# Two more units of dense matmuls ahead of the transposes of the widest attention row block, seven more ahead of the cumulative sum of the SSD decays

## The chip, the cores and the metric

The kernel runs on one core of a Trainium2 chip. The metric is the time of one execution in microseconds of the device. Before the change, three runs took 1780.59, 1785.44 and 1792.77 us; the median is 1785.44 us.

## The reference, cut to what matters

One decoder block on 512 tokens plus 16 meta tokens, width 2048. After an RMSNorm, one input projection gives q, k, v, a gate, the inputs of a state-space branch (z, x, B, C, dt) and two merge gates. Two branches run on these: differential attention with ALiBi over 8 heads, and a chunked state-space scan (SSD). They are projected, merged by gates, projected again, added to the input and normalised. The two places that this case is about:

```python
def diff_attention(q, k, v, lam):            # 8 heads, blocks of 128 rows
    ...
        s = s - (slopes[:, None, None] * dist)[None, :, None]
        s = jnp.where(valid, s, NEG)
        p = jax.nn.softmax(s, axis=-1)
        a = p[:, :, 0] - lam * p[:, :, 1]     # two maps, subtracted
        return jnp.einsum('bhqk,bkhe->bqhe', a, vf)
...
    dtf = jax.nn.softplus(dt + dt_bias[l])
    a = -jnp.exp(a_log[l])
    da = dt * a ; acs = jnp.cumsum(da, axis=-1)   # within chunks of 128, in ssd_chunked
```

## The kernel before, in words

**Dense work.** All large matrix products are cut into jobs. A job loads four weight tiles (128x1024), and most jobs use one level of Strassen: seven products P1, P6, P7, P4, P2, P3, P5 with two *units* each, so 14 units. A unit is 12 matmuls of 256 or 264 columns: each weight block is split into a high part `wh` (ACT, L194) and a rest `wl` (DVE, `split`, L190), and the products are high by high, high by low and low by high. `wh` and `wl` have five buffers each. The units go through a short pipeline: sums of weights, then the split, then, three units later (`LOOK`, L391), the matmuls.

**Side work.** Attention and the SSD scan are Python generators in the list `tasks`. After each dense unit, `run_side` (L218) advances each active generator to its next `yield`, so one `yield` is one unit of dense work between two steps. At most three are active, and a new one starts at least three units after the last one during attention. A head makes seven tasks: the transposes of v, the parts of q and k, four row blocks (`attn_rows`, i = 0 to 3; the widest, i = 3, spans 528 keys), and `attn_out`, which squares, scales and transposes the output that the row blocks left in `o_ps`. The next head's tasks follow 28 units (two jobs) behind.

**A row block** computes its scores, biases them with a running minimum (DVE), takes the two exponentials (ACT, L789), combines the two maps into `a` (DVE, L793 to L796; the tile's name in the profile is `sc`), waits three yields, and transposes `a` on TensorE (L803 to L806; `s_ps<-ident,sc`). `at` and `ax` are copied out of PSUM, and one yield later `o_ps` is accumulated.

**decays** (L917) is the only side task of the stage that projects B, C and x and runs the convolution (the conv stage, from about 577 us on). It turns dt into `dtk` by a softplus written as a series on DVE (tiles `eac`, `dec`, `dds`, `acs` of 128x160), forms `da` (stored in `dec`, L956), waits five yields, and sums it with two matmuls against `tri` and `ones` (L963, L964). In this stage each job also has conv taps on DVE (`cv<-raw`, L995; `cv<-cth`, L998).

**Order.** TensorE executes in the order in which the program is written (`InOrder`). VectorE is held to it only for the first units (`setattr(dve, "on", False)`, L698). After that the scheduler of the tile framework chooses the order of DVE, ACT, POOL and the queue SP; each engine then works off its list in order and stops at the first instruction whose inputs are missing. Weight tiles, the constants of the next stage and stores all go through SP.

Of the kernel before, what the change touches and what calls it, by code (L numbers as in the profile page):

```python
# [137 lines left out]
def block_kernel(ctx, tc, t_in, out):  # L138
# [12 lines left out]
    def side_ps():  # L151
        return pss.tile([P, 512], F32, tag="s", bufs=4, name="s_ps")
# [17 lines left out]
    for _, _, form, mat, _ in jobs:  # L170
        n = 2 if form == "A" else {"att": 2, "dt": 1}.get(mat, 4)
# [566 lines left out]
    def attn_rows(hd, i, qs, ks, kl, vt, hs):  # L738

        slope = 2.0 ** -(hd + 1)  # L740
        n = M + (i + 1) * P
        n0 = min(n, 512)
        to = P * (3 - i)
        if i == 0:
            hs["sm"] = ab.tile([P, 2, NT], F32, tag="sm", bufs=2, name="sm")
            hs["o"] = pso.tile([P, NT, P], F32, tag="o", bufs=1, name="o_ps")
        sm, o_ps = hs["sm"], hs["o"]
        mn = ab.tile([P, 4], F32, tag="mn", bufs=3, name="mn")
        pr, pq = [], {}

        def scores(*maps):
            rows = slice(i * P, (i + 1) * P)
            todo = []
            for m in maps:
                pq[m] = [side_ps(), side_ps() if n > n0 else None]
                todo += [(m, ps, a, b) for ps, a, b in ((pq[m][0], 0, max(n0, 256)), (pq[m][1], n0, n))
                         if ps is not None]
            for m, ps, a, b in todo:
                pe.matmul(ps[:, :b - a], lhsT=qs[:, m, rows], rhs=ks[:, m, a:b], start=True, stop=False)
            for m, ps, a, b in todo:  # L760
                ms = slice(64 * m, 64 * m + 64)
                pe.matmul(ps[:, :b - a], lhsT=qs[ms, m, rows], rhs=kl[ms, a:b], start=False, stop=True)

        def biased(m):
            s_ = ab.tile([P, L], F32, tag="sc", bufs=SC, name="sc")
            dve.tensor_tensor_reduce(out=s_[:, :n0], in0=pq[m][0][:, :n0], in1=tb[:, to:to + n0], scale=1.0,
                                     scalar=FAR, op0=ALU.add, op1=ALU.min, accum_out=mn[:, m:m + 1])
            if n > n0:
                dve.tensor_tensor_reduce(out=s_[:, n0:n], in0=pq[m][1][:, :n - n0], in1=tb[:, to + n0:to + n], scale=1.0,
                                         scalar=FAR, op0=ALU.add, op1=ALU.min, accum_out=mn[:, 2 + m:3 + m])  # L770
            pr.append(s_)

        if n == n0:
            scores(0, 1)
            yield
            biased(0)
        else:
            scores(0)
            yield
            biased(0)  # L780
            scores(1)
            yield
        biased(1)
        if n > n0:
            dve.tensor_tensor(mn[:, 0:2], mn[:, 0:2], mn[:, 2:4], ALU.min)
        dve.tensor_scalar(mn[:, 0:2], mn[:, 0:2], slope, None, ALU.mult)
        yield
        for m in range(2):
            act.activation(pr[m][:, :n], pr[m][:, :n], AF.Exp, scale=-slope, bias=mn[:, m:m + 1],  # L789
                           accum_out=sm[:, m, i:i + 1])  # L790
        yield
        cc = ab.tile([P, 1], F32, tag="cc", bufs=2, name="cc")
        dve.reciprocal(cc, sm[:, 1, i:i + 1])  # L793
        dve.scalar_tensor_tensor(cc, cc, nlam, sm[:, 0, i:i + 1], ALU.mult, ALU.mult)
        a = pr[0]
        dve.scalar_tensor_tensor(a[:, :n], pr[1][:, :n], cc, a[:, :n], ALU.mult, ALU.add)  # L796
        yield
        yield
        yield
        at = ab.tile([P, 4, P], F32, tag="at", bufs=1, name="at")  # L800
        ax = ab.tile([M, P], F32, tag="ax", bufs=1, name="ax")
        ps = side_ps()
        for j in range(i + 1):  # L803
            pe.transpose(ps[:, j * P:(j + 1) * P], a[:, j * P:(j + 1) * P], ident)
        pa = ps[:M, 3 * P:] if i < 3 else side_ps()[:M, :P]
        pe.transpose(pa, a[:, (i + 1) * P:n], ident)  # L806
        yield
        act.activation(at[:, :i + 1, :], ps[:, :(i + 1) * P], AF.Copy)
        dve.tensor_copy(ax, pa)
        yield  # L810
        for j in range(i + 1):
            pe.matmul(o_ps[:, i, :], lhsT=at[:, j, :], rhs=vt[:, j, :], start=(j == 0), stop=False)
        pe.matmul(o_ps[:, i, :], lhsT=ax, rhs=vt[:M, i + 1, :], start=False, stop=True)
        yield

    def attn_out(hd, sg, hs):

        for _ in range(6):
            yield
        sm, o_ps = hs["sm"], hs["o"]  # L820
        ssq = ab.tile([P, NT], F32, tag="ssq", bufs=2, name="ssq")
        r0 = ab.tile([P, NT], F32, tag="r0", bufs=2, name="r0")
        og = ab.tile([P, NT, P], F32, tag="at", bufs=1, name="og")
        for i in range(NT):
            act.activation(og[:, i, :], o_ps[:, i, :], AF.Square, accum_out=ssq[:, i:i + 1])
        dve.reciprocal(r0, sm[:, 0, :])
        yield
        dve.tensor_tensor(ssq, ssq, r0, ALU.mult)
        dve.tensor_tensor(ssq, ssq, r0, ALU.mult)
        dve.tensor_scalar(ssq, ssq, 1.0 / P, EPS, ALU.mult, ALU.add)  # L830
        pool.tensor_tensor(ssq, ssq, mhalf[:, :NT], ALU.pow)  # L831
        yield
        yield
        dve.tensor_tensor(r0, r0, ssq, ALU.mult)
        dve.tensor_tensor(og, o_ps, r0.unsqueeze(2).to_broadcast([P, NT, P]), ALU.mult)
        yield
        yield
        ps = side_ps()
        for i in range(NT):
            pe.transpose(ps[:, i * P:(i + 1) * P], og[:, i, :], ident)  # L840
        yield
        dve.scalar_tensor_tensor(sg, ps, gat, sg, ALU.mult, ALU.mult)
        sp.dma_start(d_oa[hd % 2, :, :, hd // 2].rearrange("t p n -> p t n"), sg.rearrange("p (t n) -> p t n", t=2))
        yield
# [15 lines left out]
    def head_tasks(hd, qT, kT, vT, vt, sg):  # L860
        hs = {}
        qs = ab.tile([P, 2, S], F32R, tag="qs", bufs=1, name="qs")
        ks = ab.tile([P, 2, L], F32R, tag="ks", bufs=1, name="ks")
        kl = ab.tile([P, L], F32R, tag="kl", bufs=1, name="kl")
        tasks.append(v_tokens(vT, vt))
        tasks.append(qk_parts(hd, qT, kT, qs, ks, kl))
        for i in range(NT):
            tasks.append(attn_rows(hd, i, qs, ks, kl, vt, hs))
        tasks.append(attn_out(hd, sg, hs))
# [47 lines left out]
    def decays(sb):  # L917
# [36 lines left out]
        act.activation(al, al, AF.Exp)  # L954
        da = e5
        dve.scalar_tensor_tensor(da, dtk, -1.0, al.unsqueeze(1).to_broadcast([P, 5, 32]), ALU.mult, ALU.mult)  # L956
        yield
        yield
        yield
        yield  # L960
        yield
        ps = side_ps()
        pe.matmul(ps[:, :160], lhsT=tri, rhs=da, start=True, stop=True)  # L963
        pe.matmul(ps[:, 160:320], lhsT=ones.to_broadcast([P, P]), rhs=da, start=True, stop=True)  # L964
# [17 lines left out]
    with tc.tile_pool(name="conv", bufs=2) as sb:  # L982
# [23 lines left out]
        def conv_job(ji, fts):  # L1006
# [11 lines left out]
            return strassen(ji, HL, 0, dst, fin)  # L1018

        tasks.append(decays(sb))  # L1020
        for g in range(NG):
            dense(conv_job(job_at["bc", g], [16 + g, 20 + g]))
# [448 lines left out]
```

## Time and profile before

| | before |
|---|---|
| median of three runs | 1785.44 us (1780.59 to 1792.77) |
| the profiled execution | 1787.64 us, of which the span of its instructions 1785.9 us |
| TensorE busy | 1677.5 us (94%) |
| VectorE busy | 1556.6 us (87%) |
| ScalarE busy | 962.8 us (54%) |
| granted TensorE clock, mean | 0.982 |

Busy times overlap, so they don't add up to the span. The attention stage lies at about 125 to 575 us, the conv stage at about 577 to 862 us. The waits view lists for an engine what it stood idle for; the timeline shows single instructions with the idle time before them; the windows view gives the busy time of each engine in a stretch, with the granted clock (1.00 is 2.4 GHz, 0.50 is 1.2 GHz).

### The profile page before, as it was taken

To read this page: it belongs to the slowest core of one execution; us is meant where nothing else is said; L and a number is where in the kernel's file an instruction comes from. 1 tells how busy PE (TensorE), PEld (TensorE's weight loads), DVE (VectorE), ACT (ScalarE), POOL (GpSimd) and SP (SyncE) were. 2 spreads that over 40 slices of the span, in tenths; PEclk is the share of its full clock that TensorE was granted. 3 is DMA by queue.
4 is the path that set the end of the run, shared out by engine and by line. 5 is a ranking of instruction groups with operands and counts; after the bars stand their busy time and mean duration, and the time that the engine had idled before them with its cause. 6 is when DMAs were issued, how large, how long until landed. Compare 5 with 4: busy or idle time off the path is not lost. (4 is left out here: it accounts for less than half of the span.)

```text
span 1785.9 us, 35840 instructions
## 1 busy us (share of the span) xinstructions
PE 1677.5 (94%) x13547; PEld 1622.2 (91%) x13547; DVE 1556.6 (87%) x3016; ACT 962.8 (54%) x1957; POOL 243.9 (14%) x232
## 2 busy tenths in 40 slices
PE   4999999999999799999899989999999999989996
PEld 3999988889889799999898988999998999989996
DVE  6789878888888899999798988989987499999997
ACT  5455555555565455555556656665564254456553
POOL 0000000000000000000013232323300022223443
PEclk8999999999999899999999999999999999999998
DMA  7342222222223333333455555554467544533433
GB/s 305 107 129 73 90 89 77 72 79 88 89 91 112 100 120 122 129 120 130 148 166 157 174 159 169 163 178 146 150 231 247 189 132 163 170 125 112 141 119 107
DMA packets 136765, 244.10 MB, mean 137 GB/s; under 512 B 15088, under 2 KB 78768, under 8 KB 136080
## 3 DMA queue, kind: packets, MB, share of 16 engines
q1 hardware_dynamic: 136592, 241.81, 41.9%
q8 instruction: 107, 1.75, 0.4%
q14 instruction: 66, 0.54, 0.1%
HBM read 207.88 MB, written 33.88 MB: 135 GB/s over the span
## 5 line engine op out<-in xcount | busy, mean ns | idle before, releaser
L128 PE MATMUL d_ps<-x,wh 128*128 128x256 f32 (+1 forms) x4896 | 912.9, 287 | 15.1 <-DVE cth L128 4.3
L128 PEld LDWEIGHTS d_ps<-x,wh 128*128 128x128 f32 x4896 | 764.4, 191 | 31.9 <-issue 9.3
L128 PE MATMUL d_ps<-x,wl 128*128 128x256 f32 (+1 forms) x2448 | 698.6, 285 | 17.0 <-DVE wl L128 16.5
L194 ACT ACTIVATE wh<-w 128x512 fp32r<-128x512 f32 x706 | 437.4, 627 | 395.2 <-PE d_ps L128 299.2
L128 PE MATMUL d_ps<-y,wh 128*128 128x256 f32 (+1 forms) x3216 | 600.0, 286 | 9.1 <-ACT wh L194 4.6
L128 DVE TENSOR_TENSOR wl<-w,wh 128x512 fp32r<-128x512 f32 x706 | 505.4, 727 | 105.1 <-ACT wh L194 99.6
L128 PEld LDWEIGHTS d_ps<-y,wh 128*128 128x128 f32 x3216 | 498.1, 190 | 20.3 <-issue 5.5
L128 PEld LDWEIGHTS d_ps<-x,wl 128*128 128x128 f32 x2448 | 464.9, 190 | 22.5 <-DVE wl L128 22.0
L128 PE MATMUL d_ps<-y,wl 128*128 128x256 f32 (+1 forms) x1608 | 455.7, 283 | 4.9 <-DVE wl L128 4.9
L128 PEld LDWEIGHTS d_ps<-y,wl 128*128 128x128 f32 x1608 | 303.9, 189 | 6.3 <-DVE wl L128 6.3
L194 ACT ACTIVATE wh<-S 128x512 fp32r<-128x512 f32 x260 | 160.6, 627 | 193.0 <-PE d_ps L128 111.5
L128 DVE TENSOR_TENSOR wl<-S,wh 128x512 fp32r<-128x512 f32 x260 | 182.9, 719 | 26.8 <-ACT wh L194 24.7
L128 DVE TENSOR_TENSOR S<-S,w 128x512 f32<-128x512 f32 x130 | 93.2, 753 | 0.0
L128 DVE TENSOR_TENSOR w<-w 128x512 f32<-128x512 f32 x130 | 90.8, 715 | 0.0
L128 DVE TENSOR_TENSOR w<-w,S 128x512 f32<-128x512 f32 x130 | 89.4, 699 | 0.9
L128 DVE TENSOR_TENSOR S<-w 128x512 f32<-128x512 f32 x130 | 86.3, 705 | 2.1 <-DMA w<-in_w_all 2.0
L211 POOL TENSOR_TENSOR mq<-mq,cth 128x256 f32<-128x256 f32 x32 | 43.7, 1379 | 260.8 <-ACT wh L194 144.7
L831 POOL TENSOR_TENSOR ssq<-ssq,mhalf 128x4 f32<-128x4 f32 x8 | 8.1, 1007 | 470.7 <-DVE ssq L128 470.7
L128 DVE TENSOR_TENSOR u<-d_ps,u 128x256 f32<-128x256 f32 (+1 forms) x130 | 55.2, 424 | 9.3 <-PE d_ps L128 8.8
L1117 ACT ACTIVATE mm<-mm,acs 128x128 f32<-128x128 f32 x128 | 40.1, 389 | 36.8 <-DMA mm<-d_acs 36.8
L128 DVE SCALAR_TENSOR_TENSOR cv<-raw,c_conv_w,cv 128x528 f32<-128x528 f32 x72 | 54.5, 779 | 1.1 <-issue 0.7
L211 POOL TENSOR_TENSOR state<-state,dec 128x512 f32<-128x512 f32 x12 | 19.6, 1630 | 172.3 <-DVE state L128 172.2
(233 smaller groups left out, 1524.1 us busy)
## 6 DMA issues: line engine op xcount, KB each, us to landing
w<-in_w_all SPq DMA_DIRECT2D x291, 512.0 KB, 3.6
mm<-d_acs SPq DMA_DIRECT2D x16, 512.0 KB, 6.5
d_x<-cv SPq DMA_DIRECT2D x24, 264.0 KB, 2.0
q_B<-in_xT SPq DMA_DIRECT2D x8, 528.0 KB, 11.9
d_tha<-gth SPq DMA_DIRECT2D x16, 256.0 KB, 2.4
lx<-d_x SPq DMA_DIRECT2D x16, 256.0 KB, 4.2
ea<-d_acs SPq DMA_DIRECT2D x32, 128.0 KB, 3.7
d_sz<-gth SPq DMA_DIRECT2D x16, 256.0 KB, 4.1
```

The source lines that it names most:

```text
L128: r = op(*args, **kw)
L194: act.activation(h[:, :n], src, AF.Copy)
L211: pool.tensor_tensor(dst, a, b, ALU.mult)
L831: pool.tensor_tensor(ssq, ssq, mhalf[:, :NT], ALU.pow)
L1117: act.activation(mm[:, h, :], mm[:, h, :], AF.Relu, scale=-1.0, bias=acs[:, c, g * HPG + h:g * HPG + h + 1])
```

## The change

Three numbers of yields change. In `attn_rows`, the row block i = 3 (the only one with `n > n0`) waits five units instead of three between the combination of the maps and the transposes. `attn_out` begins two units later, so that its squares stay behind the last write of `o_ps`. In `decays`, 12 units instead of 5 lie between `da` and the two matmuls. No instruction is added or taken away.

```diff
@@ attn_rows
         dve.scalar_tensor_tensor(a[:, :n], pr[1][:, :n], cc, a[:, :n], ALU.mult, ALU.add)
-        yield
-        yield
-        yield
+        for _ in range(5 if n > n0 else 3):
+            yield
@@ attn_out
-        for _ in range(6):
+        for _ in range(8):
             yield
@@ decays
         dve.scalar_tensor_tensor(da, dtk, -1.0, al.unsqueeze(1).to_broadcast([P, 5, 32]), ALU.mult, ALU.mult)
-        yield
-        yield
-        yield
-        yield
-        yield
+        for _ in range(12):
+            yield
```

What this does to the order of instructions, at three places:

TensorE, second head, around the transposes of its row block 3 (`s_ps` is the transposes' PSUM tile, `sc_2628` the combined map, `d_ps` a product of a dense unit). Before:

```order
L128 MATMUL d_ps_2747<-x_542,wh_2696 128x256
L128 MATMUL d_ps_2747<-x_541,wl_2697 128x256
L128 MATMUL s_ps_2782<-ident_139,sc_2628 128x128 x4
L128 MATMUL s_ps_2787<-ident_139,sc_2628 16x128
L128 MATMUL d_ps_2794<-x_100,wh_2725 128x264
```

Now:

```order
L128 MATMUL d_ps_2785<-x_101,wh_2743 128x264
L128 MATMUL d_ps_2785<-x_100,wl_2744 128x264
L128 MATMUL s_ps_2819<-ident_139,sc_2628 128x128 x4
L128 MATMUL s_ps_2824<-ident_139,sc_2628 16x128
L128 MATMUL d_ps_2834<-y_623,wh_2764 128x264
```

The 24 matmuls of 264 columns that read `wl_2726` and `wl_2744` stood behind the transposes and now stand ahead of them. This is the same in the heads after it.

VectorE, at the same place, up to the instruction that completes `sc_2628`. Before:

```order
L128 TENSOR_SCALAR mn_2601<-mn_2601 128x2
L128 TENSOR_TENSOR u4_2761<-d_ps_2700,u2_2547 128x256
L128 TENSOR_TENSOR wl_2765<-S_2741,wh_2764 128x512
L128 TENSOR_TENSOR wl_2791<-S_2741,wh_2790 128x512
L128 TENSOR_TENSOR sg_1961<-d_ps_2747,u3_2597 128x256
L128 TENSOR_TENSOR qT_1957<-d_ps_2747,u4_2761 128x256
L128 RECIPROCAL r0_2834<-sm_2338 128x4
L128 RECIPROCAL cc_2720<-sm_2338 128x1
L128 SCALAR_TENSOR_TENSOR cc_2720<-cc_2720,nlam_151,sm_2338 128x1
L128 TENSOR_TENSOR wl_2813<-w_2470,wh_2812 128x512
L128 SCALAR_TENSOR_TENSOR sc_2628<-sc_2664,cc_2720,sc_2628 128x528
```

Now:

```order
L128 TENSOR_SCALAR mn_2601<-mn_2601 128x2
L128 TENSOR_TENSOR u4_2761<-d_ps_2700,u2_2547 128x256
L128 TENSOR_TENSOR wl_2765<-S_2741,wh_2764 128x512
L128 RECIPROCAL r0_2875<-sm_2338 128x4
L128 RECIPROCAL cc_2720<-sm_2338 128x1
L128 TENSOR_TENSOR sg_1961<-d_ps_2747,u3_2597 128x256
L128 TENSOR_TENSOR qT_1957<-d_ps_2747,u4_2761 128x256
L128 SCALAR_TENSOR_TENSOR cc_2720<-cc_2720,nlam_151,sm_2338 128x1
L128 TENSOR_TENSOR wl_2782<-S_2741,wh_2781 128x512
L128 SCALAR_TENSOR_TENSOR sc_2628<-sc_2664,cc_2720,sc_2628 128x528
```

One split fewer stands between the scaled minimum `mn` and `sc`; on ScalarE the two exponentials of L789 stand one split earlier, right behind `wh_2764`. The heads after it show the same; the first head's order is unchanged here.

VectorE in the conv stage, the end of the softplus series up to `dec` (this is `da`) and what follows it. Before:

```order
L128 SCALAR_TENSOR_TENSOR dtk_7369<-acs_7370,dtk_7369 128x160
L128 SCALAR_TENSOR_TENSOR cv_7767<-raw_7640,c_conv_w_7377,cv_7767 128x528
L128 SCALAR_TENSOR_TENSOR cv_7815<-raw_7593,c_conv_w_7377,cv_7815 128x528
L128 COPY eac_7371<-dtk_7369 128x32
L128 SCALAR_TENSOR_TENSOR cv_7767<-cth_7768,cv_7767 128x528
L128 MEMSET dtk_7369 128x32
L128 SCALAR_TENSOR_TENSOR cv_7815<-cth_7816,cv_7815 128x528
L128 COPY dtk_7369<-eac_7371 16x32
L128 SCALAR_TENSOR_TENSOR dec_7372<-dtk_7369,c_a_log_7365 128x160
L128 COPY acs_7370<-s_ps_7699 128x160
```

Now, the last of it:

```order
L128 MEMSET dtk_7369 128x32
L128 SCALAR_TENSOR_TENSOR cv_7799<-cth_7800,cv_7799 128x528
L128 TENSOR_TENSOR wl_7854<-w_7492,wh_7853 128x512
L128 TENSOR_TENSOR S_7921<-w_7742,w_7744 128x512 x2
L128 COPY dtk_7369<-eac_7371 16x32
L128 TENSOR_TENSOR wl_7874<-w_7492,wh_7873 128x512
L128 TENSOR_TENSOR w_7742<-w_7578,w_7742 128x512 x2
L128 SCALAR_TENSOR_TENSOR dec_7372<-dtk_7369,c_a_log_7365 128x160
L128 COPY acs_7370<-s_ps_7849 128x160
```

From the sums `raw_7593` and `raw_7640`, which end the stage's first job, up to `dec`, the list had 3 splits `wl` and now has 10; it had no sum of weights (`S`, `w`) and now has 6; and it has 2 sums `u` more. Conv taps and steps of the series are the same. On TensorE the two matmuls that read `dec` stand 84 matmuls (7 units) further back; the last unit ahead of them reads `wl_7624` before and `wl_7765` now.

## Rows read from the trace of the kernel before

**Rows 1.** Waits of PE, 125 to 575 us: total us, times, longest.

```profile
PE s_ps L128 <- DVE sc L128: 17.0, 7, 2.6
```

**Rows 2.** Windows, 125 to 575 us: length, busy PE, PEld, DVE, ACT, POOL, clock, DMA.

```profile
125.00:575.00 450.00, 432.96 (x3393) 410.47 (x3392) 381.13 (x944) 249.82 (x569) 8.54 (x14) 0.99 0.27 87
```

**Rows 3.** Timeline of PE, first and second head: start, us, instruction, idle before.

```profile
176.13 0.76 PE L128 MATMUL s_ps<-ident,sc 128*128 128x128 f32 x5 [1.52 <-DVE sc L128]
...
230.59 0.77 PE L128 MATMUL s_ps<-ident,sc 128*128 128x128 f32 x5 [2.59 <-DVE sc L128]
```

**Rows 4.** Timeline of DVE, second head.

```profile
229.77 0.76 DVE L128 SCALAR_TENSOR_TENSOR sc<-sc,cc 128x528 f32<-128x528 f32 x1
...
234.03 0.69 DVE L128 TENSOR_TENSOR wl<-w,wh 128x512 fp32r<-128x512 f32 x1 [1.53 <-ACT wh L194]
```

**Rows 5.** Timeline of ACT, second head.

```profile
226.54 0.63 ACT L194 ACTIVATE wh<-S 128x512 fp32r<-128x512 f32 x1 [0.78 <-DVE wl L128]
227.08 0.72 ACT L789 ACTIVATE sc<-sc,mn 128x528 f32<-128x528 f32 x1
```

**Rows 6.** Windows behind the waits of the second, third and fourth head.

```profile
231.00:237.00 6.00, 6.00 (x38) 5.77 (x36) 2.74 (x5) 2.14 (x4) 0.00 (x0) 0.72 0.19 49
286.00:292.00 6.00, 5.47 (x33) 5.39 (x34) 3.07 (x6) 2.07 (x4) 0.00 (x0) 0.72 0.00 0
343.00:349.00 6.00, 6.00 (x49) 5.76 (x47) 2.93 (x7) 3.28 (x12) 0.00 (x0) 1.00 0.27 85
```

**Rows 7.** Windows of the conv stage.

```profile
580.00:600.00 20.00, 20.00 (x168) 19.82 (x167) 18.45 (x42) 10.17 (x21) 0.00 (x0) 1.00 0.36 121
600.00:611.00 11.00, 1.24 (x7) 1.05 (x6) 9.54 (x23) 3.48 (x6) 0.20 (x2) 0.68 0.27 92
611.00:620.00 9.00, 9.00 (x65) 8.95 (x64) 3.84 (x8) 3.81 (x8) 0.00 (x0) 0.83 0.26 76
...
640.00:860.00 220.00, 213.75 (x1749) 211.48 (x1747) 219.26 (x424) 116.78 (x198) 1.81 (x18) 1.00 0.37 127
```

**Rows 8.** Waits of PE, 575 to 870 us.

```profile
PE s_ps L128 <- DVE dec L128: 9.8, 1, 9.8
PE d_ps L128 <- DVE wl L128: 6.9, 8, 1.5
```

**Rows 9.** Timeline of PE, the matmuls of `decays`.

```profile
582.33 0.44 PE L128 MATMUL s_ps<-ident,dtx 32*16 32x32 f32 x5
...
600.09 0.28 PE L128 MATMUL d_ps<-x,wl 128*128 128x264 f32 x1
610.14 0.87 PE L128 MATMUL s_ps<-dec,tri 128*128 128x160 f32 x2 [9.76 <-DVE dec L128]
```

**Rows 10.** Timeline of DVE ahead of `dec` and behind it.

```profile
597.37 0.69 DVE L128 TENSOR_TENSOR wl<-w,wh 128x512 fp32r<-128x512 f32 x1
597.97 1.29 DVE L128 TENSOR_TENSOR S<-S,w 128x512 f32<-128x512 f32 x2
599.17 0.43 DVE L128 TENSOR_TENSOR u<-d_ps,u 128x264 f32<-128x264 f32 x1
600.41 0.50 DVE L128 TENSOR_TENSOR raw<-d_ps,u 128x8 f32<-128x8 f32 x2 [0.57 <-PE d_ps L128]
...
609.67 0.33 DVE L128 SCALAR_TENSOR_TENSOR dec<-dtk,c_a_log 128x160 f32<-128x160 f32 x1
...
635.44 2.13 DVE L128 SCALAR_TENSOR_TENSOR cv<-raw,c_conv_w,cv 128x528 f32<-128x528 f32 x3 [0.38 <-ACT cv L1001]
```

**Rows 11.** Timeline of SP's queue at the end of the attention stage.

```profile
571.77 0.38 SPq L843 DMA_DIRECT2D d_oa<-sg  x1
...
574.46 0.33 SPq L453 DMA_DIRECT2D c_ssm_g<-in_ssm_g  x1
...
577.21 0.43 SPq L920 DMA_DIRECT2D dtx<-d_dt  x1
```

**Rows 12.** DMA issues, 570 to 580 us: size, us to landing.

```profile
dtx<-d_dt SPq DMA_DIRECT2D x1, 66.0 KB, 1.9
```

## The prediction

> **What bounds the kernel now.** The page's first part comes first: TensorE is busy 94% of the span, VectorE 87%. So time can come only from stretches in which TensorE stands still or is slowed, and only if VectorE is not itself the limit there. The waits of TensorE, stage by stage, then name the two waits that the change aims at. In the attention stage there is one kind of wait only: the transposes wait for `sc`, 17.0 us in 7 waits [rows 1]. The windows view shows VectorE busy for 381 of these 450 us, so it has slack there [rows 2]. In the conv stage the matmuls that read `dec` wait 9.8 us once, and eight waits for `wl` make 6.9 us [rows 8]. There VectorE has no slack: it is busy 219.3 of 220 us from 640 us on [rows 7]. The two stages must therefore be costed differently: in the first a wait that goes is time won, in the second only what VectorE gains as well.
>
> **Term 1, the transposes of row block 3.** The timeline shows the waits: 1.52 us in the first head, 2.59 us in the second [rows 3]; with 17.0 in all, five more of about 2.58. The eighth head has none. In the second head TensorE is out of work at 230.59 - 2.59 = 228.00. A unit takes 20.00 us / 14 = 1.43 us (168 matmuls of 264 columns are 14 units [rows 7]), so the two units that now stand ahead keep it busy until 230.86. VectorE began the last step of `sc` at 229.77 and ended it at 230.53 [rows 4], 0.33 us before that. The order makes the margin larger, not smaller: the exponentials began at 227.08, behind a split of 0.63 us that began at 226.54 [rows 5] and that now follows them, and one split fewer stands ahead of `sc` on VectorE. I therefore take the whole 17.0 us. The splits that feed the two units were done before the transposes in the old order too, so the units don't start a wait of their own. Bounds: 17.0 if all go, 8 if VectorE, which no longer catches up during the stalls, is late at half of the places. I take the upper end because VectorE stood idle for 1.53 us right after the stall, waiting for ScalarE and not for time of its own [rows 4].
>
> **Term 2, the clock behind these waits.** Behind the waits of the second and third head the granted clock averages 0.72 over 6 us, at the level of 1.2 GHz for part of it; behind the fourth head's it stays at 1.00 [rows 6]. What it costs is 6 x 0.28 = 1.7 us a time; from the third head's I take 1.6, since its window begins inside the wait. Together 3.3 us. With no stall in the stage I expect the clock to stay up, so these come back. Bounds: 0 to 3.3, as other executions may have fewer or more such falls. The Trainium skill, page "TensorE: Matmul & The Clock Gate", section "HAM oscillation — how this bites in real kernels", says that only long idle gaps throttle the array again, so waits this short should cost nothing beside themselves; by it this term is 0. The trace disagrees in two of the seven waits, and the rows decide.
>
> **Term 3, the matmuls on `dec`.** They now stand 7 units = 7 x 1.43 = 10.0 us later on TensorE, against a wait of 9.76 us [rows 9]. Taken alone that would close the wait. But VectorE was busy throughout that wait: it went from the sums `raw` at 600.41, where it had just caught up (0.57 us idle), to `dec` at 609.67 [rows 10]. In that time it made the splits of the next three units only. The order now puts 7 more splits, 6 more sums of weights and 2 more `u` ahead of `dec`. One split takes 0.60 us from start to start, two sums 1.20, a `u` at most 0.43 [rows 10]: 7 x 0.60 + 6 x 0.60 + 2 x 0.43 = 8.7 us more on VectorE ahead of `dec`. So `dec` comes 8.7 us later while TensorE arrives 10.0 us later. The wait shrinks only from 9.8 to 9.76 - 10.0 + 8.7 = 8.5 us, and the gain is 1.3 us. The clock falls again behind so long a wait: 0.83 over 9 us now [rows 7], 1.5 us, which stays. The splits that are done beforehand then let VectorE rest, but not lead: it is limited by the five buffers of `wl` and `wh`, and at the first conv taps of the next job (635.44, 0.38 us idle [rows 10]) it has caught up in either case. From there on it is saturated and the stage runs as before. Bounds: a gain of 9.8 + 1.5 = 11.3 if the wait and its clock fall go altogether, a loss of 2 if the weight tiles that the 6 sums read land late. I take 1.3, because the lists of both engines give it.
>
> **Term 4, the end of the attention stage.** `attn_out` ends two units = 2.9 us later, the last head's with it. Its store was issued at 571.77; the constants of the next stage begin on SP's queue at 574.46 and `dtx`, last of them, at 577.21 [rows 11], landing 1.9 us later [rows 12], at 579.1. TensorE reads it at 582.33 [rows 9]. Of the 3.2 us of slack 0.3 is left. The weight tile queued behind `dtx` has long slack too, as the queue then stands at stores of the gates. VectorE scales the first constant soon after that store and may idle for about a microsecond; I charge 0.5 us, with bounds of 0 and 2.
>
> Nothing else is moved off cover: the earlier heads' output tasks run beside the next head's units as before, three or more units from their next reader.
>
> **Sum.** 17.0 + 3.3 + 1.3 - 0.5 = 21.1 us. The profiled execution took 1787.64 us (span 1785.9, and 1.7 around it), so it would take 1766.5. It lies 2.2 us above the median of the runs; on the median's scale the forecast is 1785.44 - 21.1 = **1764 us**.
>
> **Rivals.**
> - *The wait on `dec` goes too* (12%). If the lists matter less than I think and VectorE reaches `dec` by the time of the matmul, term 3 is 11.3 and the time 1785.4 - 31.1 = 1754. For it: seven units are longer than the wait. Against it: 8.7 us of VectorE work are put ahead, on an engine without idle time there.
> - *Part of the stalls come back in the attention stage* (16%). VectorE loses 17 us in which it caught up; the waits then appear at `wl` or stay at the transposes. With term 1 at 8 and term 2 at half, the gain is 8 + 1.7 + 1.3 - 0.5 = 10.5 and the time 1775. For it: VectorE is busy 381 us, and the stage shrinks from 450 to 430. Against it: 49 us of idle time are left.
> - *No clock comes back* (10%). Five of the seven waits left the clock alone, so a typical execution may have no fall to lose. The gain is 17.0 + 1.3 - 0.5 = 17.8 and the time 1768. The rule of the clock page quoted above would make this the outcome.
> - *The waits move instead of going, and the kernel gets slower* (4%). If `sc` were later by as much as the transposes are moved, each head would still stall, and if all seven stalls then fell to the lower clock, five more falls of 1.65 us cost 8 us: 1794. It decides from the point where VectorE ends `sc` 2.9 us later than now, at 233.4 in the second head. The order, with one split less ahead of it, speaks against it.
> - *A new wait elsewhere eats all* (4%): 1785. That the change doesn't do what it says is excluded for TensorE by its order.
>
> My forecast itself has 54%.
>
> **How the numbers follow.** The time is that of the forecast, 1764. The range runs from 1752, just past the first rival, to 1777, just past the second, and leaves out the last two rivals and the tails of the others, some 16%. One per cent, 17.9 us, is about what a measurement can tell from no change; the line is at 1767.6. The forecast lies below it with 85% of its 54%, the first rival wholly, the clock rival with half: 0.63 faster. The rest within 1% is 0.33, slower 0.04.
>
> **What would show it.** Term 1: the waits of TensorE from 125 to 555 us list no wait for `sc`, or less than 2 us. Term 2: the clock of that stretch is 1.00. Term 3: the wait on `dec` is still there, at 7 to 9 us, with the seven splits ahead of it on VectorE; if it is under 3 us, term 3 is wrong. Term 4: TensorE waits under 1 us for `dtx`. The prediction fails altogether if waits for `wl` of more than 5 us appear in the attention stage.

## The result

The changed kernel takes 1767.03 us, the median of four runs from 1761.83 to 1771.03; the kernel before took 1785.7 on the same chip. The ratio is 0.9882, with a 95% interval of 0.9862 to 0.9903: 21.1 us less, 17.3 to 24.6. The two medians differ by 18.7, which lies in that interval. The forecast was 1764, in a range of 1752 to 1777. The profiled execution of the changed kernel is the shortest of its four, 1761.83 us (span 1760.0), and that of the kernel before lay 2.2 us above its median, so the difference of the two profiles, 25.8 us, is more than the result.

The page's first part, of the changed kernel:

```profile
span 1760.0 us, 35816 instructions
PE 1671.6 (95%) x13547; PEld 1618.2 (92%) x13547; DVE 1556.0 (88%) x3016; ACT 961.3 (55%) x1957; POOL 240.3 (14%) x232
```

**The attention stage.** The list of TensorE's waits from 125 to 575 us is empty now; in [rows 1] it held 17.0 us. The windows of the changed kernel over the same stretch and over those of [rows 2, 6] (length, busy PE, PEld, DVE, ACT, POOL, clock, DMA share, GB/s):

```profile
125.00:575.00 450.00, 450.00 (x3569) 428.69 (x3569) 400.12 (x990) 261.29 (x594) 9.19 (x14) 1.00 0.29 93
231.00:237.00 6.00, 6.00 (x49) 5.74 (x48) 4.87 (x13) 3.32 (x14) 1.01 (x1) 1.00 0.55 175
286.00:292.00 6.00, 6.00 (x52) 5.98 (x52) 5.30 (x13) 3.26 (x8) 1.01 (x1) 1.00 0.22 78
```

TensorE is busy without a gap, at a clock of 1.00 throughout. VectorE has 400 of 450 us of work in this stretch, where it had 381: the same time now holds more of the program. In the second head ScalarE's exponentials, VectorE's last step of `sc` and TensorE's transposes lie like this (timelines of ACT, DVE and PE, one row of each):

```profile
223.20 0.73 ACT L789 ACTIVATE sc<-sc,mn 128x528 f32<-128x528 f32 x1
```

```profile
226.97 0.76 DVE L128 SCALAR_TENSOR_TENSOR sc<-sc,cc 128x528 f32<-128x528 f32 x1
```

```profile
228.29 0.71 PE L128 MATMUL s_ps<-ident,sc 128*128 128x128 f32 x5
```

`sc` is finished at 227.73, and the transposes begin at 228.29 with no idle time ahead of them, where they had waited 2.59 us [rows 3]. The margin is 0.56 us.

**The end of that stage.** SP issues the load of `dtx` at 557.70, 19.5 us earlier than before [rows 11]. It lands 2.0 us later, and TensorE's transposes of it, one group of five matmuls, begin 0.7 us after that without a wait. The issue (timeline of SP's queue) and the matmuls (view of the tile `dtx`: shortest, median and longest ns; first and last start):

```profile
557.70 0.43 SPq L919 DMA_DIRECT2D dtx<-d_dt  x1
```

```profile
L128 PE MATMUL s_ps<-ident,dtx x5: 192/222/223, 560.4 to 560.6; 32*128 32x32 f32 x4, 32*16 32x32 f32 x1
```

**The conv stage.** TensorE's waits of the changed kernel from 560 to 870 us (total, times, longest), and the timeline of PE at `dec`:

```profile
PE s_ps L128 <- DVE dec L128: 7.9, 1, 7.9
PE d_ps L128 <- DVE wl L128: 6.1, 7, 1.5
PE d_ps L128 <- ACT wh L194: 3.8, 1, 3.8
```

```profile
596.47 0.87 PE L128 MATMUL s_ps<-dec,tri 128*128 128x160 f32 x2 [7.92 <-DVE dec L128]
```

The wait on `dec` is still there, 7.9 us instead of 9.8 [rows 8, 9]. The one for `wh` is not new: it stands at 849.88, and the kernel before has its counterpart of 2.9 us just behind 870. VectorE's timeline on both sides of `dec`:

```profile
594.21 0.67 DVE L128 TENSOR_TENSOR wl<-w,wh 128x512 fp32r<-128x512 f32 x1
594.81 1.27 DVE L128 TENSOR_TENSOR w<-w 128x512 f32<-128x512 f32 x2
596.02 0.31 DVE L128 SCALAR_TENSOR_TENSOR dec<-dtk,c_a_log 128x160 f32<-128x160 f32 x1
597.91 0.33 DVE L128 COPY acs<-s_ps 128x160 f32<-128x160 f32 x1 [1.59 <-PE s_ps L128]
...
603.50 0.69 DVE L128 TENSOR_TENSOR wl<-S,wh 128x512 fp32r<-128x512 f32 x1 [1.75 <-ACT wh L194]
```

Splits and sums of weights run right up to `dec`. Behind it VectorE rests for 1.59 us, until the matmuls on `dec` are done, and for 1.75 us, until ScalarE has made the next `wh`. The windows of the changed kernel around it, which answer to [rows 7]:

```profile
588.00:597.00 9.00, 1.08 (x7) 0.90 (x6) 8.32 (x18) 2.55 (x4) 0.20 (x2) 0.73 0.26 88
597.00:606.00 9.00, 9.00 (x56) 8.95 (x55) 4.63 (x12) 2.90 (x6) 0.00 (x0) 0.70 0.08 33
606.00:616.00 10.00, 10.00 (x85) 10.00 (x85) 8.04 (x16) 6.03 (x10) 0.00 (x0) 1.00 0.18 59
616.00:836.00 220.00, 213.78 (x1751) 211.73 (x1750) 218.90 (x422) 115.37 (x195) 1.81 (x18) 1.00 0.38 127
```

VectorE's idle time from 588 to 616 us is 0.68 + 4.37 + 1.96 = 7.0 us; from 616 on it is busy 218.9 of 220. TensorE's clock behind the wait is 0.70 over 9 us, where it was 0.83 [rows 7].

The trace's clock records show why. While TensorE stood waiting, the granted clock fell to 0.50, at 603.89 before the change and at 592.14 in the changed kernel; it came back to 1.00 at 614.13 and 602.38, an equally long stretch. The shorter wait covers less of it, so more of it falls on matmuls. These are the windows from the end of the wait to the rise, the first of the kernel before, the second of the changed one:

```profile
610.14:614.13 3.99, 3.99 (x17) 3.99 (x18) 0.98 (x3) 0.60 (x3) 0.00 (x0) 0.50 0.27 100
596.47:602.38 5.91, 5.91 (x26) 5.91 (x27) 2.17 (x6) 1.16 (x3) 0.00 (x0) 0.50 0.20 79
```

Taken at half, that is 2.0 us lost before and 3.0 now (an estimate): of the 1.8 us by which the wait shrank, about 1.0 is given back at the lower clock. In e8, the changed kernel once more, the clock fell earlier in the wait and 4.8 us of the stretch were left behind it.

**Where the 25.8 us of the two profiles lie.** The matmuls on `d_ps` stand in nearly the same order in both kernels, so the start of the n-th of them can be subtracted. The changed kernel is 0.8 us ahead when the attention stage begins and 22.0 ahead at its end: 21.2 us come from there. At the end of the conv stage (the 5,500th, 845.85 against 822.90) it is 22.9 ahead: 1.0 us more. The last 2.8 to 3.0 arise behind 860 us, where nothing was changed. There the clock falls in some places, in different ones in each execution; experiments e7 and e8 below show how much this part differs between two executions of one kernel.

The 1.0 us of the conv stage is small, so it needs the other profiles beside it. Between the same two matmuls (the end of the attention stage and the 5,500th), e7, e1 and e4, which have the old `decays`, gain 0.1, 0.8 and -0.4 us on the first profile of the kernel before; the changed kernel, e8 and e2, which have the new one, gain 1.0, 1.5 and 1.4. The new `decays` are thus worth about one microsecond here, hardly more than two executions differ by.

### The profile page after: what moved, and what is told of

It reads as the page before. It is cut to its first block, busy times and chain, and to the rows that moved or that the text cites. A ratio compares the mean times of both kernels' runs of the same rounds, so it can differ in the third digit from the quotient of the medians.

```text
span 1760.0 us, 35816 instructions
## 1 busy us (share of the span) xinstructions
PE 1671.6 (95%) x13547; PEld 1618.2 (92%) x13547; DVE 1556.0 (88%) x3016; ACT 961.3 (55%) x1957; POOL 240.3 (14%) x232
## 3 DMA queue, kind: packets, MB, share of 16 engines
q8 instruction: 107, 1.75, 0.4%
## 4 chain that ended last, share of the span: by engine, by line
PE 68%; DVE 15%; issue 6%; DMA 5%; ACT 4%; POOL 1%; SPq 0%; DVEq 0%; ACTq 0%; POOLq 0%
PE d_ps L128 61%; PE s_ps L128 6%; DVE wl L128 4%; DMA mm<-d_acs 3%; DVE cv L128 2%; PE o_ps L128 2%; DVE S L128 2%; ACT mm L1113 1%; DVE w L128 1%; ACT wh L194 1%; DVE u L128 1%; DVE y L128 1%; DVE res L128 1%; DVE mm L128 1%; DMA d_yg<-lz 0%
```

## The experiments

Two theories stood against each other for each half of the change. Attention: the stalls go whole because `sc` isn't late by itself, or part of them comes back. Conv stage: `dec` is late because the order on VectorE puts other work ahead of it (then few of the yields help), or because the cover is too short (then more of it helps in proportion). A third question was the clock: whether its falls belong to a place in the program or to an execution. "Before" is always the kernel before on the same chip.

**e1, the attention part alone** (against the changed kernel):

```
-        for _ in range(12):
+        for _ in range(5):
```

> The attention part alone (row block 3 waits five units, attn_out begins two units later; decays as in the kernel before). Theory of the prediction: the seven waits on sc (17.0 us) and the clock falls behind two of them (3.3 us) go, minus up to 0.5 us at the end of the attention stage: about 20 us under the kernel before, and the wait on dec stays at 9 to 10 us. Rival (the decays carry the gain): under 12 us, with waits for wl or for the transposes in the attention stage. Rival (no clock comes back): 17 us.

It took 1769.16 us, ratio 0.99 (0.9885 to 0.9915). From 125 to 575 us no wait is listed and the clock is 1.00. The same matmuls gain 21.2 us over the attention stage, as in the full change. The wait on `dec` is 9.8 us again. The window of the attention stage, and two waits from 560 to 870 us:

```profile
125.00:575.00 450.00, 450.00 (x3569) 428.73 (x3569) 400.04 (x990) 260.32 (x592) 9.20 (x14) 1.00 0.29 93
```

```profile
PE s_ps L128 <- DVE dec L128: 9.8, 1, 9.8
PE d_ps L128 <- DVE wl L128: 7.3, 8, 1.7
```

By its time, 17.9 us less (15.2 to 20.5), e1 lies nearer the rival without the clock (17) than the theory's 20; the stage, with its clock of 1.00 and its 21.2 us, tells them apart. Nearly all of the gain is the attention part's.

**e2, the conv part alone** (against the kernel before, in place of the five yields of `decays`):

```
-        yield
-        yield
-        yield
-        yield
-        yield
+        for _ in range(12):
+            yield
```

> The decays part alone (12 units instead of 5 ahead of the matmuls on dec; attention as in the kernel before). Theory of the prediction (VectorE's list puts 8.7 us more work ahead of dec): the wait on dec is 8 to 9 us instead of 9.8, and the time falls by 0 to 2 us; the seven waits on sc stay at 17 us. Rival (seven units of cover are worth their time): the wait is under 2 us and the time falls by 8 to 11 us.

It took 1784.95 us, ratio 0.9991 (0.9982 to 1.0), 0 to 3 us less. The two waits, one listed from 125 to 575 us and one from 560 to 870:

```profile
PE s_ps L128 <- DVE sc L128: 17.0, 7, 2.6
...
PE s_ps L128 <- DVE dec L128: 7.9, 1, 7.9
```

The seven waits on `sc` stay to the tenth, the wait on `dec` shrinks to 7.9 us as in the full change, just under the 8 to 9 forecast, and the conv stage is 1.4 us shorter. The two parts add: 17.9 and 1.6 by the ratios, against 21.1 for both, within the intervals.

**e3, twice the cover ahead of `dec`** (against the changed kernel):

```
-        for _ in range(12):
+        for _ in range(24):
```

> The changed kernel with 24 instead of 12 units ahead of the matmuls on dec. On VectorE's list dec now stands 3 splits behind TensorE's place instead of 5 ahead of it, and from 18 units on nothing more is put ahead of it. Both theories: no wait on dec. Theory that VectorE bounds this stage: against the changed kernel only VectorE's idle time of this stretch can be won, 4 to 7 us, and waits for wl come in place of part of the wait. Rival (TensorE bounds it): the whole wait and the clock fall behind it, 9 to 11 us.

It took 1755.64 us, ratio 0.9829 (0.9815 to 0.9842): by the ratios 9.5 us less than the change as made. No wait on `dec` is left. TensorE's waits from 560 to 870 us, and two windows:

```profile
PE d_ps L128 <- DVE wl L128: 8.4, 11, 1.5
PE d_ps L128 <- ACT wh L194: 2.6, 1, 2.6
PE d_ps L128 <- DVE dtk L128: 0.5, 1, 0.5
```

```profile
588.00:606.00 18.00, 17.21 (x141) 16.79 (x139) 18.00 (x40) 9.96 (x18) 0.20 (x2) 1.00 0.29 96
...
616.00:836.00 220.00, 212.04 (x1732) 209.59 (x1732) 219.27 (x424) 115.59 (x197) 1.60 (x16) 1.00 0.38 127
```

VectorE has hardly any idle time left behind 588 us, and the waits for `wl` have grown by 2.3 us. Counted from the end of the attention stage, the same matmuls are 11.1 us earlier than in the changed kernel right behind `dec`, and 8.2 at the end of the conv stage (the 5,500th). The wait and its clock fall, 7.9 + 2.7 = 10.6 us on TensorE, are thus first won whole. 2.4 of them are given back later, about as much as the waits for `wl` grew; VectorE had only 7.0 us of rest to give. The stage's 8.2 lies between the 4 to 7 of the first theory and the 9 to 11 of the rival: neither account alone is right.

**e6, 18 yields:**

```
-        for _ in range(12):
+        for _ in range(18):
```

> The changed kernel with 18 units ahead of the matmuls on dec. The list of VectorE grows by 4 splits and one pair of sums raw (0.60 each and 0.8: 3.2 us) ahead of dec, TensorE's arrival moves by 6 units (8.6 us). Theory (wait = work ahead of dec on VectorE less the units of cover): the wait is 7.9 + 3.2 - 8.6 = 2.5 us. Rival (the scheduler follows any cover): it stays at 7 to 9 us. Rival (no wait beyond the cover of 10 us): none.

Its one run took 1758.09 us, and the wait on `dec` is 1.1 us, where the arithmetic gave 2.5:

```profile
PE d_ps L128 <- DVE wl L128: 7.9, 11, 1.5
PE d_ps L128 <- ACT wh L194: 2.7, 1, 2.7
PE s_ps L128 <- DVE dec L128: 1.1, 1, 1.1
```

The step from 12 to 18 yields takes 6.8 us off the wait, the step from 5 to 12 only 1.8. Both engines' shares can be read from the traces, on the scale of the shifted program. `dec` is 3.2 us later than with 12 yields, as forecast; but TensorE arrives 10.0 us later instead of 8.6. Of the 1.4 us more, 0.8 are two new waits for `wl` ahead of `dec`, where the changed kernel has none (waits from 575 to 598 us); the other 0.6 have no row of their own:

```profile
PE d_ps L128 <- DVE wl L128: 0.8, 2, 0.5
```

The price in the list is thus not a fixed share: the first seven yields put 8.3 us of work ahead of `dec`, the next six 3.2. And a part of the shorter wait is only moved to `wl`.

**e5, the list itself.** The attention part with five yields, but VectorE keeps the operations of `decays` in the order of the program instead of sorting them in by due time (against the changed kernel):

```
         dve.memset(x5, 0.0)
+        dve.on = True
...
-        for _ in range(12):
+        for _ in range(5):
...
+        dve.on = False
         dve.tensor_copy(acs, ps[:, :160])
```

> The attention part of the change and only five units ahead of the matmuls on dec, but VectorE is held to the program's order from the start of decays to those matmuls, so that no split that is written later stands ahead of dec (2 splits behind TensorE's place instead of 5 ahead). Theory (the scheduler's list makes dec late, not too few units): the wait on dec is under 2 us with the old cover of five units, and the time is 7 to 11 us below that of the attention part alone (1769), 1758 to 1762. Rival (five units are too few, whatever the list): the wait stays at 8 to 10 us and the time at 1769. Rival (order written by hand makes VectorE wait for ScalarE elsewhere): no wait on dec, but 5 us or more of waits for wl in its place and no gain.

It took 1758.39 us, ratio 0.9852 (0.9833 to 0.9871). With no more cover than the kernel before had, the wait on `dec` is gone: VectorE makes `dec` at 574.20, and TensorE reads it at 577.98.

```profile
577.98 0.43 PE L128 MATMUL s_ps<-dec,tri 128*128 128x160 f32 x2
```

```profile
PE d_ps L128 <- DVE wl L128: 10.6, 12, 1.8
PE d_ps L128 <- ACT wh L194: 2.9, 1, 2.9
PE d_ps L128 <- ACT c L302: 0.3, 1, 0.3
```

The conv stage ends up 6.1 us shorter than in the changed kernel. With the other work gone from ahead of `dec` on VectorE the old cover is enough. That doesn't make it the only way: more cover alone removes the wait too (e3), and wins 2.1 us more of the stage.

**e9 and e10, both ways together, and e3 once more.** e9 is the changed kernel (12 yields) with the two added lines of e5; e10 is e3 again.

> The changed kernel (12 yields) with VectorE's operations of decays kept in the order of the program, so that dec is early in its list and TensorE late at its reader. Theory (once TensorE no longer waits for dec, VectorE's own work is the limit of the conv stage, and neither more cover nor an earlier dec brings more): no wait on dec, VectorE busy 99% or more of 588 to 836 us, waits for wl of 8 to 10 us, the conv stage 8 us shorter than in the changed kernel as with 24 yields, and a time within 4 us of that kernel's, 1752 to 1760. Rival (the two ways add, the earlier dec also feeding the splits sooner): waits for wl under 5 us and the stage 10 us or more shorter, a time under 1752.

> The changed kernel with 24 yields once more, beside the run before it on the same chip. Both theories: no wait on dec, waits for wl of about 8.4 us, VectorE without idle time from 588 to 606 us, 1755.6 us, give or take 4 for falls of the clock that differ by execution.

e10 took 1755.43 us, ratio 0.9823 (0.9807 to 0.984); its waits for `wl` are 8.9 us in 12, and VectorE is busy 18.00 of 18.00 us from 588. e9 took 1759.97, ratio 0.9849 (0.9831 to 0.9867). The two ways don't add, so the rival falls; but the theory also missed, on the waits for `wl`, on VectorE's share and on the length of the stage. In e9 the operations that follow `dec` are kept in order too, and from 592.76 to 597.16 conv steps, parts of `decays` and sums run with no split among them. TensorE then waits 1.88 us for `wl`. Its timeline, TensorE's waits from 560 to 870 us, and the windows behind it:

```profile
597.89 0.39 PE L128 MATMUL d_ps<-x,wl 128*128 128x264 f32 x1 [1.88 <-DVE wl L128]
```

```profile
PE d_ps L128 <- DVE wl L128: 12.1, 15, 1.9
```

```profile
598.00:606.00 8.00, 7.06 (x36) 6.75 (x37) 7.83 (x14) 2.88 (x6) 0.00 (x0) 0.58 0.28 100
606.00:616.00 10.00, 10.00 (x84) 10.00 (x84) 8.45 (x17) 5.83 (x10) 0.00 (x0) 0.99 0.38 127
```

The clock behind it is 0.58 over 8 us, 3.4 us of TensorE's time, and VectorE then idles 1.73 us for a matmul. The stage ends 3.1 us shorter than in the changed kernel, against 8.2 in e3 and e10; the 1.9 of this wait and the 3.4 at the lower clock are about the 5.1 between them. That only the order behind `dec` costs this wasn't run by itself.

**e4, a smaller cover in the attention stage** (against the changed kernel, with the five yields of `decays`):

```
-        for _ in range(5 if n > n0 else 3):
+        for _ in range(4 if n > n0 else 3):
...
-        for _ in range(8):
+        for _ in range(7):
...
-        for _ in range(12):
+        for _ in range(5):
```

> One unit instead of two moved ahead of the transposes (row block 3 waits four units, attn_out begins one unit later; decays as in the kernel before). Theory of the prediction: a unit is 1.43 us, so waits of 2.59 shrink by 1.43 and by what the shorter list ahead of sc saves (0.6 to 1.4 us): 0 to 0.6 us each stay, 0 to 4 us in all, and the time falls by 15 to 20 us. Rival (the list alone, not the cover, removes the waits): nothing is left of them. Rival (a short wait costs the clock as well): the waits that stay are followed by the lower clock and the time falls by less than 12 us.

It took 1772.76 us, ratio 0.9917 (0.9903 to 0.993). TensorE's waits from 125 to 575 us, and the second head:

```profile
PE s_ps L128 <- DVE sc L128: 4.8, 6, 0.9
```

```profile
228.57 0.77 PE L128 MATMUL s_ps<-ident,sc 128*128 128x128 f32 x5 [0.80 <-DVE sc L128]
```

Six waits of 0.8 us instead of 0 to 0.6: a miss by 0.2 each. The time falls by 14.8 us by the ratio, just under the 15 to 20 forecast. One unit of 1.43 us takes about 1.7 off the longest wait, and the second is needed for the rest. The clock is 1.00 in all of the stage.

**e7 and e8, both kernels once more**:

> The kernel before once more, for a second profile. Theory (whether a wait of 2.6 us costs the clock depends on the execution): seven waits of 17.0 us in all again, but the lower clock behind other or more or fewer of them than the second and third head's; the falls between 860 and 1260 us also differ. Rival (the place in the program decides): the same two falls.

> The changed kernel once more, for a second profile. Theory: 1765 to 1771 us; wait on dec 7.9 us, no wait on sc, no fall of the clock from 60 to 555 us, but more falls between 860 and 1260 us than the none of the first profile, which was the shortest of its four runs. Rival (the change itself took the falls of that stretch away): none again, and 1762 us.

e7 took 1793.38 us, e8 1763.42, one run each; e8 is below the 1765 to 1771 that was expected of it. The windows of e7 behind the waits of the second, third and fourth head, to be held against [rows 6]:

```profile
231.00:237.00 6.00, 6.00 (x36) 5.76 (x36) 2.26 (x4) 2.28 (x7) 0.00 (x0) 0.73 0.27 70
286.00:292.00 6.00, 6.00 (x39) 5.80 (x39) 2.89 (x6) 2.14 (x4) 0.00 (x0) 0.76 0.02 6
343.00:349.00 6.00, 6.00 (x49) 5.76 (x48) 2.54 (x8) 3.34 (x13) 0.29 (x1) 1.00 0.25 87
```

The falls stand behind the same two of the seven waits; in e2 the three windows give 0.72, 0.72 and 1.00. The theory that these falls differ by execution is wrong for the attention stage. For the stages behind 860 us it holds. The windows from 860 to 1560 us, of the changed kernel's two profiles:

```profile
860.00:1560.00 700.00, 675.38 (x5598) 653.50 (x5597) 611.97 (x1075) 380.74 (x791) 146.66 (x120) 1.00 0.55 173
```

```profile
860.00:1560.00 700.00, 676.26 (x5580) 654.70 (x5579) 609.76 (x1072) 379.14 (x789) 146.69 (x120) 0.99 0.54 172
```

By the trace's clock records TensorE stood at the lower level for 3.4 us of this stretch in the first and 13.7 in the second; in the two profiles of the kernel before it was 17.1 and 27.3, in e1 23.9, in e5 6.8. Up to half of each is lost time. So the 2.8 to 3.0 us by which the first two profiles differ behind 860 us can't be put down to the change.

## Why the prediction was right

**Term 1, the transposes (17.0 us): right.** All seven waits are gone, and no other takes their place. The margin in the second head was forecast as more than 0.33 us and is 0.56. The rival in which part of the stalls comes back falls: VectorE's 49 us of slack were enough. e4 shows how near it was, since one unit fewer already leaves 4.8 us.

**Term 2, the clock (3.3 us): right, and better founded than I knew.** I bounded it by 0 because falls might be chance; three profiles with the waits have the same two falls, and the profiles without them have none here. The rule of the Trainium skill, page "TensorE: Matmul & The Clock Gate", section "HAM oscillation — how this bites in real kernels", by which waits this short cost nothing beside themselves, is contradicted in the second and third head and holds in the other heads. Terms 1 and 2 make 20.3 us; the stage gave 21.2. The 0.9 between them has no row of its own, and its cause stays open.

**Term 3, the matmuls on `dec` (1.3 us): right in its mechanism, with two sizes off.** TensorE arrives 10.1 us later relative to the shifted program, as forecast (10.0), and `dec` is 8.3 us later (8.7). The wait is 7.9 instead of the 8.5 forecast. That the list on VectorE causes this was an argument; e5 shows it. The larger error is the clock fall behind the wait: I took 1.5 us, "which stays", but it didn't stay. Over the same kind of window, 0.70 over 9 us is 2.7, since the stretch at the lower clock kept its length while the wait that covered part of it got shorter. The two errors, 0.6 us more off the wait and 1.2 us more at the lower clock, pull against each other; that the stage's gain (1.0 in this profile, 1.5 in e8) lies near 1.3 is in part luck. The bound I gave for the wait's full removal, 11.3, is refuted as a gain of the stage: with the wait and its fall gone, e3 and e10 end the stage 9.2 us ahead of the kernel before, 8.2 ahead of the changed one, and about 2 us come back as waits for `wl`.

**Term 4, the load of `dtx` (-0.5 us): no cost is seen.** TensorE doesn't wait. I had 0.3 us of slack left; it read the tile 0.7 us after it landed.

**The rivals.** That the wait on `dec` would go too at 12 yields is refuted by the 7.9 us that are left of it. The clock rival (1768, a gain of 17.8) lies nearer to the measured median of 1767.03 than the forecast does, and both gains lie in the interval, so the time can't tell them apart; the windows of the attention stage can, and the rival falls there.

**The number.** That the ratio gives the very 21.1 us of the sum is luck in the last microsecond or two: its interval is 7 us wide, the medians give 18.7, and the two stages of the profiles give 21.2 + 1.0 = 22.2.

**A version that beats both** is e3, run twice: 1755.6 and 1755.4 us, 30.5 and 31.7 us by the ratios below the kernel before.

## What to carry to other kernels

Cover placed ahead of an in-order wait is worth its length minus what the scheduler thereby puts ahead of the producer; so read the producer's list as well as the waiter's. If the producer's engine has no idle time, its place in that list is a second way to the same end: here it removed the wait with the old cover (6.1 us of the stage), while more than twice the cover won 8.2. Where that engine has slack, as VectorE had in the attention stage, enough cover removes the stall whole and the clock fall behind it as well: here one unit left 0.8 us a time and two left none. Where a wait is only shortened, ask how much of the lower clock behind it the wait had covered, since that part comes back. Once the wait is gone, the gain ends where the saturated engine has no rest left: add up its idle time in the stretch beforehand. In this one case the gain, 8.2 us, came out between that idle time, 7.0, and the waiter's account, 10.6.

## What was not expected of the hardware

Of seven waits of TensorE in one stage, one of 1.52 us and six of about 2.58, two were followed by a fall of the clock (0.72 to 0.76 over 6 us), the same two in three profiles; behind the others it stayed at 1.00. A wait of 1.88 us in e9, which came 2.4 us after one of 0.30 us, was followed by 0.58 over 8 us; in e5 one of 1.75 us was followed by 1.00 over 8 us (timeline of PE and the window behind it):

```profile
595.66 0.39 PE L128 MATMUL d_ps<-x,wl 128*128 128x264 f32 x1 [1.75 <-DVE wl L128]
```

```profile
596.00:604.00 8.00, 7.31 (x61) 7.10 (x60) 8.00 (x16) 2.56 (x5) 0.00 (x0) 1.00 0.35 111
```

The time at the lower level from 860 to 1560 us differed from 3.4 to 13.7 us between two executions of the same kernel, so a difference of a few microseconds between two profiles must be placed in its stage before it is put down to a change.
